# Storing GpSimd's FFN blocks from GpSimd's own DMA queue, in a two-layer hybrid trunk

## The chip, the cores and the metric

The kernel runs on one core of one Trainium2 chip. The metric is the device time of one execution in microseconds, as the median of several runs; lower is better. The core has TensorE (matmuls), VectorE, ScalarE and GpSimd, called PE, DVE, ACT and POOL in the profile, and SyncE (SP), which computes nothing and issues DMAs from its queue in order.

## The reference, cut to what matters

Two decoder layers work on x of 1024 tokens by 1024 channels, in float32. Each has a mixer (layer 0: Mamba-2 heads and latent attention; layer 1: gated linear attention and sparse attention) and then the feed-forward network (FFN) which the change touches:

```python
FFN_HIDDEN = -(-8 * D_MODEL // (3 * 256)) * 256      # 2816

def swiglu(h, w_gate, w_up, w_down):
    return (jax.nn.silu(h @ w_gate) * (h @ w_up)) @ w_down

for layer in range(DEPTH):
    ...
    h = rmsnorm(x, pre_f) * (1.0 + scale_f) + shift_f
    x = x + gate_f * rmsnorm(swiglu(h, *ffns[layer]), post_f)
```

## The kernel before, in words

**Precision.** Each float32 operand of a large product is split into a high and a low part, and a product is three matmuls (`mm3`, L111 to L116): high by high, high by low, low by high. A "product" below is twelve matmuls: four slices of the contraction, three each.

**The FFN's first half** (`ffn`, L1285). Gate and up (`mt` 0 and 1) are multiplied by the seven-product scheme of Strassen and Winograd over quarters: 2816 hidden rows are eleven pairs of 128 (`pm` 0 to 10, `NM` is 11), and each pair has seven products, named "1" to "7", for each of gate and up. They run in the order 1, 6, 2, 7, 5, 4, 3, gate before up in each. For the first five pairs (`HEADS`) products 1 and 2 are taken earlier, and their u blocks wait in DRAM (`uq`), so later those pairs take only ten products each, the others fourteen.

**Weights.** `advance`, called ahead of each product, does what is due. It loads raw weights (`load`, L1347: tiles `rawa`, four buffers, and `raw`, two buffers, the latter for the "b" half), forms their sums on VectorE (`presum`, L1353 to L1355, and one more at L1369), and splits them into high and low (`wpair`, L1333 on ScalarE and L1334 on VectorE). A `raw` buffer comes free when L1334 has read its last weight.

**Results.** A product ends in a PSUM bank, which VectorE adds to a block of 128 by 512 (tile `blk`, ten buffers): L1530, L1535, L1545, L1555 and L1565 for products 6, 7, 4, 5 and 3. SiLU is on ScalarE (L1547, L1557, L1567), and gate times up of products 4 and 5 on GpSimd (L1549, L1559). After product 3 of up, `finish` (L1483) makes the last four blocks with five operations (L1489, L1491, L1493, L1495, L1497), on GpSimd for all pairs but the last, on VectorE for the last. Each finished block is stored to the DRAM tensor `hid`, seven blocks a pair: block 0 at L1396 (made by VectorE), block 1 at L1550, block 4 at L1560, and four in `store` (L1486) in `finish`.

**The second half** (`ffn_out`, L1603) is also in seven passes. It reads `hid` back block by block (L1635) with quarters of the down weight (L1636); what it needs of sums of the down weight is formed in the first half by `down_sums`, a background stream.

**Order.** The program is written for a tile framework, which works out the semaphores and the buffers. A planner orders each engine's instructions ahead of time, by the order of the program and its own estimate of when each could start; on the chip each engine's queue then runs strictly in that order. SP's queue holds all loads and stores, so what stands behind a store waits until that store's block is made. Background streams (the modulation vectors, L257 and L276, and `down_sums`) are pinned to the order of the program.

Of the kernel before, what the change touches and what calls it, by code (L numbers as in the profile page):

```python
# [46 lines left out]
class Trunk:  # L47
# [1237 lines left out]
    def ffn(self, l, near, far, ew):  # L1285


        nc, I, m = self.nc, self.I, self.mod
        S = self.S
        tt, ptt = nc.vector.tensor_tensor, nc.gpsimd.tensor_tensor  # L1290
        hid = self.t(self.dram, [7, self.NM, P, 512], "hid")
# [12 lines left out]
        def product(ps, w, c, b, start):  # L1304

            for k in range(4):
                cs = slice(c * 512 + k * P, c * 512 + (k + 1) * P)
                self.mm3(ps, w[0][:, cs], w[1][:, cs], b[0][:, k, :], b[1][:, k, :], start and k == 0, k == 3, True)
# [71 lines left out]
        def first(mt, pm, w):  # L1380

            ps = self.cx()
            product(ps, w, 0, B[0], True)
            u = blk()
            nc.scalar.copy(u, ps)  # L1385
            return ps, u

        def second(mt, pm, w, ps):

            product(ps, w, 1, B[1], False)  # L1390
            if mt == 0:
                c = cblk[pm] = blk()
                nc.scalar.activation(c, ps, AF.Silu)
            else:
                tt(cblk[pm], cblk[pm], ps, op=ALU.mult)
                nc.sync.dma_start(hid[0, pm], cblk.pop(pm) if pm < self.HEADS else cblk[pm])  # L1396
# [32 lines left out]
        def wkey(pm, mt, p):  # L1429
            return pm, mt, "h" if pm < self.HEADS and p in "12" else WT[p]  # L1430
# [17 lines left out]
        def advance(t):  # L1448

            while loads and free[home(*loads[0])]:  # L1450
                free[home(*loads[0])] -= 1
                load(*loads.pop(0))
            def presums():
                while sums and need[sums[0][1], sums[0][0], 1] - t <= 10:
                    mt, pm = sums[0]
                    if (mt, pm, "b") not in raws or pm >= self.HEADS and (pm, mt, 0) not in W:
                        break
                    presum(*sums.pop(0))

            presums()  # L1460
            while todo and need[todo[0]] - t <= 6:
                place = places[turns[0]]
                if place in user and last[user[place]] >= t:
                    break
                pm, mt, j = key = todo[0]
                if j == "h":
                    if (mt, pm, "h") not in raws:
                        break
                elif (mt, pm, "a") not in raws or j and (mt, pm) in sums:
                    break  # L1470
                todo.pop(0)
                user[place] = key
                W[key] = prep(mt, pm, j)
                if j == 0:
                    presums()
                if j == 2:
                    free["b"] += 1
                if j == 3:
                    free["a"] += 1
                if j == "h":  # L1480
                    free[home(mt, pm, j)] += 1

        def finish(pm, g, u, u3, c21):  # L1483

            def store(n, v):
                nc.sync.dma_start(hid[n, pm], v)  # L1486
            ptt = tt if pm == self.NM - 1 else nc.gpsimd.tensor_tensor
            h11, h21, h22, h12 = cblk.pop(pm), c21, u3, u
            ptt(h12, h12, g["u"], op=ALU.mult)  # L1489
            s1, s2, s3 = g["u"], g["c21"], g["u3"]  # L1490
            ptt(s1, h12, h22, op=ALU.add)  # L1491
            store(5, s1)
            ptt(s2, s1, h11, op=ALU.subtract)  # L1493
            store(2, s2)
            ptt(s3, h11, h12, op=ALU.subtract)  # L1495
            store(3, s3)
            ptt(h12, h21, s2, op=ALU.subtract)  # L1497
            store(6, h12)

        def reload(pm):  # L1500
            for mt in range(2):
                u = ublk[mt, pm] = blk()
                nc.sync.dma_start(u, uq[mt, pm])
# [4 lines left out]
        for t, (pm, mt, p) in enumerate(seq):  # L1508
            advance(t)
            if t > 16 and t % 4 == 0:  # L1510
                self.pump()
            if len(seq) - t in (7, 6, 5, 4, 2):
                next(out)
            st = state.setdefault((pm, mt), {})
            w = W.get(wkey(pm, mt, p))
            if p == "1":
                st["x"], u = first(mt, pm, w)
                if pm < self.HEADS:
                    nc.sync.dma_start(uq[mt, pm], u)
                else:  # L1520
                    ublk[mt, pm] = u
            elif p == "2":
                second(mt, pm, w, st["x"])
                if mt and pm == self.HEADS - 1:
                    reload(0)
            elif p == "6":
                ps = self.sm()
                product(ps, w, 0, T["2"], True)
                u = ublk[mt, pm]
                tt(u, u, ps, op=ALU.add)  # L1530
            elif p == "7":
                ps = st["z"] = self.bk()
                product(ps, w, 1, T["3"], True)
                st["u3"] = blk()
                tt(st["u3"], ublk[mt, pm], ps, op=ALU.add)  # L1535
            elif p == "4":
                if mt == 0 and pm < self.HEADS:
                    cblk[pm] = blk()
                    nc.sync.dma_start(cblk[pm], hid[0, pm])
                if mt and pm + 1 < self.HEADS:  # L1540
                    reload(pm + 1)
                ps = st["z"]
                product(ps, w, 1, T["4"], False)
                c = st["c21"] = blk()
                tt(c, ublk[mt, pm], ps, op=ALU.add)  # L1545
                if mt == 0:
                    nc.scalar.activation(c, c, AF.Silu)  # L1547
                else:
                    ptt(c, c, state[pm, 0]["c21"], op=ALU.mult)  # L1549
                    nc.sync.dma_start(hid[1, pm], c)  # L1550
            elif p == "5":
                ps = st["v"] = self.bk()
                product(ps, w, 0, T["1"], True)
                c = st["u3"]
                tt(c, c, ps, op=ALU.add)  # L1555
                if mt == 0:
                    nc.scalar.activation(c, c, AF.Silu)  # L1557
                else:
                    ptt(c, c, state[pm, 0]["u3"], op=ALU.mult)  # L1559
                    nc.sync.dma_start(hid[4, pm], c)  # L1560
            else:
                ps = st["v"]
                product(ps, w, 0, T["b"], False)
                u = ublk[mt, pm]
                tt(u, u, ps, op=ALU.add)  # L1565
                if mt == 0:
                    nc.scalar.activation(u, u, AF.Silu)  # L1567
                    state[pm, 0]["u"] = u
                else:
                    g = state.pop((pm, 0))  # L1570
                    finish(pm, g, u, st["u3"], st["c21"])
                    state.pop((pm, 1))
            if t in (0, 2, 4, 6, 8, 9, 12, 16):
                next(gen)
# [928 lines left out]
```

## Time and profile before

| what | value |
|---|---|
| median of 3 runs | 3119.78 us |
| lowest and highest of them | 3115.93 and 3125.87 us |
| the profiled execution's own time | 3123.05 us |
| its span, from first to last instruction | 3121.3 us |
| mean granted TensorE clock in it | 0.985 |

The profiled execution lies 3.27 us above the median and within the runs shown; 1.75 us of its time lie outside the span. Durations in the next sections come from that one execution. In timelines a row has the start and the length in microseconds, then engine, line, operation and tiles written and read; "[2.77 <-DVE blk L1535]" says that the engine was idle 2.77 us before the row and what ended it. "q" behind an engine's name is its queue, which waits and issues DMAs. Rows of waits say who waited for whom, the total in microseconds, how often, and the longest.

### The profile page before, as it was taken

What the parts mean: (1) busy time and instruction counts of PE and PEld (TensorE: products, weight loads), DVE (VectorE), ACT (ScalarE), POOL (GpSimd) and SP (SyncE); (2) the same over time, 40 slices, a digit from 0 to 9 for tenths busy, and PEclk for the clock granted to TensorE, in tenths of its full rate; (3) what the DMA queues carried; (4) which work ended last, traced back from release to release, by engine and by line L of the source; (5) the groups of instructions that cost most, each with busy time, mean ns of one, the idle gap of its engine ahead of it and who ended that gap; (6) DMA issues with size and microseconds to landing.
All of it is one profiled execution on the core that took longest, in us unless ns stands there. A gap on an engine that the chain in (4) does not pass through costs nothing. (4 is left out here: it accounts for less than half of the span.)

```text
span 3121.3 us, 43059 instructions
## 1 busy us (share of the span) xinstructions
PE 3009.7 (96%) x15880; PEld 2437.7 (78%) x15880; DVE 2161.1 (69%) x3381; ACT 1338.6 (43%) x2193; POOL 699.0 (22%) x671
## 2 busy tenths in 40 slices
PE   7999999999999999999999999899999999999998
PEld 6887877777787888887888888767777787888787
DVE  5876856768777787667546554687766887777655
ACT  6445444546522223435432432355555732223433
POOL 1003343101034222001213422022222124222001
PEclk9999999999999999999999999999999999999999
DMA  6567432325554556974434334331313645455864
GB/s 224 167 213 223 146 119 96 101 68 197 186 176 159 195 197 234 317 253 153 147 109 156 129 103 133 117 112 57 97 51 105 234 162 195 175 190 198 291 195 161
DMA packets 222866, 510.16 MB, mean 163 GB/s; under 512 B 23824, under 2 KB 62832, under 8 KB 221632
## 3 DMA queue, kind: packets, MB, share of 16 engines
q1 hardware_dynamic: 222656, 507.42, 48.6%
q8 instruction: 125, 2.05, 0.3%
q14 instruction: 85, 0.70, 0.1%
HBM read 370.09 MB, written 137.25 MB: 163 GB/s over the span
## 5 line engine op out<-in xcount | busy, mean ns | idle before, releaser
L115 PE MATMUL bk<-slab,whi 128*128 128x512 f32 x1176 | 467.3, 397 | 1.9 <-DVE slab L145 1.9
L114 PE MATMUL bk<-slab,whi 128*128 128x512 f32 x752 | 312.4, 415 | 6.7 <-ACT whi L132 5.5
L116 PE MATMUL bk<-slab,wlo 128*128 128x512 f32 x752 | 298.1, 397 | 0.0
L115 PEld LDWEIGHTS bk<-slab,whi 128*128 128x128 f32 x1176 | 224.2, 191 | 50.8 <-issue 2.9
L114 PE MATMUL bk<-T,whi 128*128 128x512 f32 x528 | 210.0, 398 | 2.9 <-DVE blk L1535 1.7
L116 PE MATMUL bk<-T,wlo 128*128 128x512 f32 x528 | 207.7, 393 | 0.0
L151 POOL TENSOR_SCALAR rstd<-ss 128x1 f32<-128x1 f32 (+1 forms) x86 | 28.9, 336 | 712.0 <-ACT junk L158 651.7
L114 PEld LDWEIGHTS bk<-slab,whi 128*128 128x128 f32 x752 | 144.7, 192 | 41.3 <-issue 6.2
L116 PEld LDWEIGHTS bk<-slab,wlo 128*128 128x128 f32 x752 | 144.3, 192 | 31.4
L1333 ACT ACTIVATE whi<-rawa 128x512 fp32r<-128x512 f32 (+1 forms) x108 | 80.4, 750 | 194.0 <-PE bk L115 160.8
L114 PE MATMUL cx<-slab,whi 128*128 128x512 f32 x368 | 146.2, 398 | 6.5 <-ACT blk L1385 3.9
L2316 POOL TENSOR_SCALAR pexp<-pexp,rs 128x640 f32<-128x640 f32 (+7 forms) x128 | 95.8, 752 | 246.2 <-DVE rs L2315 91.5
L115 PE MATMUL cx<-slab,whi 128*128 128x512 f32 x368 | 145.1, 394 | 0.2 <-DVE slab L397 0.2
L116 PE MATMUL cx<-slab,wlo 128*128 128x512 f32 x368 | 144.9, 394 | 0.0
L1116 PE MATMUL sm<-ident,pexp 128*128 128x128 f32 x816 | 132.4, 278 | 7.1 <-POOL pexp L2316 2.3
L1559 POOL TENSOR_TENSOR blk<-blk,blk 128x512 f32<-128x512 f32 x22 | 35.3, 1602 | 419.2 <-DVE blk L1555 306.9
L1116 PEld LDWEIGHTS sm<-ident,pexp 128*128 128x128 f32 x816 | 93.4, 140 | 44.9 <-issue 19.7
L1118 ACT COPY pT<-sm 128x512 f32<-128x512 f32 (+2 forms) x144 | 76.4, 531 | 112.5 <-PE sm L1116 111.4
L1334 DVE TENSOR_TENSOR wlo<-rawa,whi 128x512 fp32r<-128x512 f32 (+1 forms) x108 | 118.1, 1094 | 7.3 <-ACT whi L1333 6.7
L114 PEld LDWEIGHTS bk<-T,whi 128*128 128x128 f32 x528 | 99.2, 188 | 28.7 <-DVE blk L1535 2.2
L2312 ACT ACTIVATE pexp<-pexp,nm 128x640 f32<-128x640 f32 (+7 forms) x128 | 94.0, 734 | 61.5 <-DVE nm L2310 46.3
L1650 DVE TENSOR_TENSOR slab<-ab,slab 128x1024 fp32r<-128x1024 f32 x66 | 80.7, 1223 | 54.1 <-ACT slab L1649 51.8
(660 smaller groups left out, 8590.2 us busy)
## 6 DMA issues: line engine op xcount, KB each, us to landing
ada<-in_l_ada_w_dram SPq DMA_DIRECT2D x80, 512.0 KB, 4.4
hid<-blk SPq DMA_DIRECT2D x154, 256.0 KB, 2.0
raw<-in_l_w_in_dram SPq DMA_DIRECT2D x48, 512.0 KB, 3.6
ab<-hid SPq DMA_DIRECT2D x94, 256.0 KB, 2.7
cat<-cat SPq DMA_DIRECT2D x64, 256.0 KB, 2.7
ab<-wt SPq DMA_DIRECT2D x60, 256.0 KB, 5.4
raw<-in_l_w_gate_dram SPq DMA_DIRECT2D x28, 512.0 KB, 4.9
raw<-in_l_w_up_dram SPq DMA_DIRECT2D x28, 512.0 KB, 4.1
```

The source lines that it names most:

```text
L114: mm(out, lh, rh, start=start, stop=False, skip_group_check=more)
L115: mm(out, lh, rl, start=False, stop=False, skip_group_check=more)
L116: mm(out, ll, rh, start=False, stop=stop, skip_group_check=more)
L151: nc.gpsimd.tensor_scalar(r, ss, inv_d, EPS, op0=ALU.mult, op1=ALU.add)
L1116: nc.tensor.transpose(ps[:, k * P:(k + 1) * P], e[:, (b + k) * P:(b + k + 1) * P], self.ident)
L1118: (nc.scalar.copy if self.evac else nc.vector.tensor_copy)(pt[:, b:b + m, :], ps[:, :m * P].rearrange("p (k c) -> p k c", c=P))
L1333: nc.scalar.activation(hi, src, AF.Copy)
L1334: (eng or nc.vector).tensor_tensor(lo, src, hi.bitcast(F32), op=ALU.subtract)
L1559: ptt(c, c, state[pm, 0]["u3"], op=ALU.mult)
L1650: tt(lo, r, hi.bitcast(F32), op=ALU.subtract)
L2312: nc.scalar.activation(e, e, AF.Exp, bias=nm, scale=-1.0, accum_out=rs)
L2316: nc.gpsimd.tensor_scalar(e, e, rs, 0.0, op0=ALU.mult, op1=ALU.add)
```

## The change

Stores of blocks that GpSimd makes are issued by GpSimd itself and no longer by SP: in `finish` for all pairs but the last, whose blocks VectorE makes and SP still stores, and at products 4 and 5 of up for every pair. Block 0 stays on SP. No arithmetic changes. Line numbers behind it rise by three.

```diff
         def finish(pm, g, u, u3, c21):
 
+            on_vector = pm == self.NM - 1
+            queue = nc.sync if on_vector else nc.gpsimd
+
             def store(n, v):
-                nc.sync.dma_start(hid[n, pm], v)
-            ptt = tt if pm == self.NM - 1 else nc.gpsimd.tensor_tensor
+                queue.dma_start(hid[n, pm], v)
+            ptt = tt if on_vector else nc.gpsimd.tensor_tensor
...
                     ptt(c, c, state[pm, 0]["c21"], op=ALU.mult)
-                    nc.sync.dma_start(hid[1, pm], c)
+                    nc.gpsimd.dma_start(hid[1, pm], c)
...
                     ptt(c, c, state[pm, 0]["u3"], op=ALU.mult)
-                    nc.sync.dma_start(hid[4, pm], c)
+                    nc.gpsimd.dma_start(hid[4, pm], c)
```

## The prediction

> **What bounds the kernel now.** I read the page first, then the windows of the two FFN product stages, then TensorE's own gaps inside them, and last what VectorE and the SP queue waited for just before each gap. The page:
>
> ```profile
> PE 3009.7 (96%) x15880; PEld 2437.7 (78%) x15880; DVE 2161.1 (69%) x3381; ACT 1338.6 (43%) x2193; POOL 699.0 (22%) x671
> ...
> q1 hardware_dynamic: 222656, 507.42, 48.6%
> ...
> hid<-blk SPq DMA_DIRECT2D x154, 256.0 KB, 2.0
> ```
>
> TensorE is busy 96% of the span, so a stall elsewhere counts only where it reaches TensorE. All the program's own DMAs run on one hardware queue; 154 of them store an FFN block. The change moves 124 of these. The windows (span, then PE, PEld, DVE, ACT, POOL busy, clock, DMA share) of the two stages in which those stores are made:
>
> ```profile
> 850.00:1210.00 360.00, 355.86 (x1526) 285.74 (x1524) 278.34 (x327) 103.33 (x145) 118.38 (x70) 1.00 0.52 182
> 2490.00:2870.00 380.00, 374.23 (x1610) 302.51 (x1609) 299.78 (x345) 113.75 (x158) 118.75 (x70) 1.00 0.52 180
> ```
>
> TensorE is idle 4.1 us in the first and 5.8 us in the second: 9.9 us together. Closing gaps can win no more in these stages, but for what a gap does to the matmuls behind it. TensorE's own timeline (start, length, idle before it) has the gaps:
>
> ```profile
> 957.32 0.50 PE L114 MATMUL bk<-T,slab 128*128 128x512 f32 x1 [2.77 <-DVE blk L1535]
> ...
> 2587.12 0.40 PE L115 MATMUL bk<-slab,whi 128*128 128x512 f32 x1
> 2587.35 0.39 PE L116 MATMUL bk<-T,wlo 128*128 128x512 f32 x1
> 2589.49 0.50 PE L114 MATMUL bk<-T,whi 128*128 128x512 f32 x1 [1.74 <-DVE blk L1535]
> ...
> 2620.94 0.50 PE L114 MATMUL bk<-T,slab 128*128 128x512 f32 x1 [3.29 <-DVE blk L1535]
> ...
> 2622.39 0.63 PE L116 MATMUL bk<-T,slab 128*128 128x512 f32 x1
> 2622.82 0.63 PE L114 MATMUL bk<-T,slab 128*128 128x512 f32 x1
> ```
>
> Matmuls normally start 0.23 us apart (2587.12, 2587.35). Three gaps, all released by L1535, VectorE's reading of a finished bank. After the last one they start 0.43 us apart (2622.39, 2622.82). Now why L1535 was late, in VectorE's timeline at the three places:
>
> ```profile
> 949.66 1.18 DVE L1334 TENSOR_TENSOR wlo<-rawa,whi 128x512 fp32r<-128x512 f32 x1
> 954.53 0.69 DVE L1353 TENSOR_TENSOR raw<-raw 128x512 f32<-128x512 f32 x1 [3.69 <-DMA raw<-in_l_w_up_dram]
> ...
> 2570.65 1.21 DVE L1334 TENSOR_TENSOR wlo<-raw,whi 128x1024 fp32r<-128x1024 f32 x1
> ...
> 2580.33 0.68 DVE L1334 TENSOR_TENSOR wlo<-rawa,whi 128x512 fp32r<-128x512 f32 x1
> 2587.41 0.69 DVE L1353 TENSOR_TENSOR raw<-raw 128x512 f32<-128x512 f32 x1 [6.41 <-DMA raw<-in_l_w_up_dram]
> 2588.14 0.69 DVE L1354 TENSOR_TENSOR rawa<-raw,rawa 128x512 f32<-128x512 f32 x1
> 2588.75 0.68 DVE L1535 TENSOR_TENSOR blk<-blk,bk 128x512 f32<-128x512 f32 x1
> ...
> 2613.18 1.19 DVE L1334 TENSOR_TENSOR wlo<-rawa,whi 128x512 fp32r<-128x512 f32 x1
> 2618.14 0.69 DVE L1353 TENSOR_TENSOR raw<-raw 128x512 f32<-128x512 f32 x1 [3.77 <-DMA raw<-in_l_w_up_dram]
> ```
>
> Each time VectorE stands, 3.7 to 6.4 us, at the first of the weight sums (L1353) for an up weight that has not landed, and L1535 is queued behind it. The SP queue at the same places (start, length; merged rows hold several stores):
>
> ```profile
> 944.67 5.97 SPq L1486 DMA_DIRECT2D hid<-blk  x4
> 950.73 0.38 SPq L1347 DMA_DIRECT2D raw<-in_l_w_up_dram  x1
> ...
> 2569.55 0.33 SPq L1347 DMA_DIRECT2D raw<-in_l_w_gate_dram  x1
> 2575.28 5.44 SPq L1486 DMA_DIRECT2D hid<-blk  x4
> ...
> 2581.29 0.39 SPq L1347 DMA_DIRECT2D raw<-in_l_w_up_dram  x1
> ...
> 2608.20 5.97 SPq L1486 DMA_DIRECT2D hid<-blk  x4
> 2614.26 0.38 SPq L1347 DMA_DIRECT2D raw<-in_l_w_up_dram  x1
> ```
>
> The load goes out right behind the four stores of `finish`. At the middle place its buffer was free when VectorE had read the last weight out of it, 2570.65 + 1.21 = 2571.86, but it was issued at 2581.29: 9.4 us late, while SP stood at stores whose blocks GpSimd had not finished. What SP waited for in the first stage (us in total, times, longest):
>
> ```profile
> SPq L1486 <- POOL blk L1491: 59.8, 10, 8.0
> SPq L1550 <- POOL blk L1549: 37.0, 10, 5.1
> SPq L1560 <- POOL blk L1559: 34.5, 10, 6.3
> ```
>
> **The change part by part.** *Stores taken off SP.* Per layer: four in `finish` for ten of eleven blocks and one each at the two products for all eleven, 62, so 124. SP saves 124 issues of 0.32 us (row below), 40 us, and waits like the three rows above, 131 us in one stage. Neither is on the path by itself; SP is no bound. What counts is the load behind: the three L1353 waits go if it lands 3.7 to 6.4 us sooner, and at the middle place there are 9.4 us to take.
>
> *TensorE's three gaps.* By starts less the normal 0.23: the first counts as its idle 2.77 plus about 0.16 of modelled overlap, 2.9; the second 2589.49 - 2587.35 - 0.23 = 1.9; the third 3.29 plus the same 0.16, 3.45. Behind the third, some seven matmuls at 0.43 instead of 0.23: 1.4. Sum 9.7 us: 7.8 of the 9.9 idle, 0.5 of overlap and the 1.4; the other 2.1 of idle have other causes and stay.
>
> *What is late next.* With the weight there, VectorE goes on at once. Three sums at about 0.69 and L1535 at 0.68 make 2.75 us. At the middle place: 2581.01 + 2.75 = 2583.8, and TensorE wants it at 2587.58; 3.8 to spare. At the first: 950.84 + 2.75 = 953.6, wanted at 957.32 - 2.93 = 954.4; 0.8 to spare. At the last: 2614.37 + 2.75 = 2617.1, wanted at 2620.94 - 3.45 = 2617.5; 0.4 to spare. So they close, the last just so. I take 9 of the 9.7.
>
> *Stores put on GpSimd's queue.* No DMA is issued by GpSimd in this trace. The nearest rows, a store from SP, and GpSimd's own pass over one block (ns, least/median/most), then GpSimd's chain in `finish` (first and last of five) and a later row of VectorE:
>
> ```profile
> L1486 SPq DMA_DIRECT2D hid<-blk x88: 319/320/459, 883.3 to 2904.9; - x88
> L1559 POOL TENSOR_TENSOR blk<-blk,blk x22: 1281/1308/2237, 868.4 to 2890.7; 128x512 f32<-128x512 f32 x22
> ...
> 2570.87 2.15 POOL L1489 TENSOR_TENSOR blk<-blk,blk 128x512 f32<-128x512 f32 x1 [3.63 <-DVE blk L1565]
> ...
> 2578.74 1.63 POOL L1497 TENSOR_TENSOR blk<-blk,blk 128x512 f32<-128x512 f32 x1
> ...
> 2597.05 0.68 DVE L1545 TENSOR_TENSOR blk<-blk,bk 128x512 f32<-128x512 f32 x1
> ```
>
> An issue costs GpSimd between 0.32 and 2.24 us; I take 1.0, between them, since it must wait for its own last write as well as issue. GpSimd has 118.38 busy in 360; 60 stores add 19 to 134 us, and it stays under 71%. So no bound. Behind a store on this queue stand only GpSimd's later passes, and for their results nothing waits but stores and the reuse of the ten `blk` buffers. The chain of `finish` takes 2580.37 - 2570.87 = 9.5 us; with four issues 10.8 to 18.5, plus 2.0 to land. One block later, seven blocks are held from the old one and nine are asked for up to L1545 at 2597.05, 26.2 us after the chain began; the last is asked for 5.7 us after the worst case. Cost 0; if an issue took over 3.7 us, VectorE would wait there.
>
> A page bears on this price: the Trainium skill, DMA: Bandwidth & Descriptors, section Latency and other measured facts, gives about 1 us to the first byte on the GpSimd path and 0.6 on SP's. By it the sum would not change; no run here shows it yet.
>
> *The other stores.* hid[0], the spare u blocks and all of the last block's four stay on SP. The last block's two product stores move; they are read only in the second and later of the seven passes behind. Cost 0.
>
> *Order.* The planner sets the order of every queue from its own estimate, and GpSimd's longer chain changes what it sees, in the FFN and behind. No row prices that. The gaps it could open are like those seen, 1.9 to 3.5 us each; one or two either way, minus 5 to plus 5. I take 0.
>
> Sum against the profiled execution: 3123.05 - 9 = 3114. That execution lies 3.3 us above the median of 3119.78, so against the median it is 3111. I forecast 3112.
>
> **The rivals.**
>
> *Nothing moves.* Loads land sooner, but something else stands in front of L1535: the sums have 0.4 and 0.8 us to spare at two of three places, and a SP wait for another buffer could take the place of the stores. Then at most the middle gap closes, 2 us: 3118. The Trainium skill speaks for this case: DMA: Bandwidth & Descriptors, section Issuing engines are not separate DMA queues, says that starting DMAs from several engines only saves the time to start them, usually small. By that rule the gain would be the 0.32 us issues, which are off the path: 3120. The rows above disagree as far as they go, as what SP lost was not issue time but 59.8 us at one wait.
>
> *Slower: GpSimd's issues hold VectorE up.* The two engines already disturb each other:
>
> ```profile
> L1369 DVE TENSOR_TENSOR rawa<-raw,rawa x44: 676/694/1789, 837.9 to 2859.5; 128x512 f32<-128x512 f32 x44
> ...
> sum 120.00, PE 114.93 PEld 91.79 DVE 97.08 ACT 28.93 POOL 49.57; mean PE 38.31 PEld 30.60 DVE 32.36 ACT 9.64 POOL 16.52
> ```
>
> One VectorE sum takes 0.69 us, or up to 1.79 beside a GpSimd pass. If a store's issue cost VectorE the same 1.1, six stores add 6.6 us for each block. The second row sums 2540 to 2660, the part in which five blocks take ten products of twelve matmuls each, 27.6 us: VectorE has 114.93 - 97.08 = 17.9 to spare there, 4.1 per block. So TensorE would lose 2.5 for each of ten such blocks, 25, and the gaps that close give back 9: 3119.8 + 16 = 3136. It decides from 0.7 us a store (4.1 / 6) upward; it is slower than now from about 0.85, and by over 0.3% from 1.0. Against it: an issue does not read the blocks, the pass does. The Trainium skill (SBUF: State Buffer, section Who interferes with whom) has VectorE's sums of two inputs contend only with GpSimd instructions that read; the two lengths of L1369 agree with the first half, and of the second no row here can tell.
>
> *More than forecast.* SP's earlier issue also brings the loads of the next stage forward; worth perhaps 5 us more: 3107.
>
> **How the numbers follow.** Gaps close: 0.50, around 3112, its own range 3107 to 3117. Nothing moves: 0.28. Slower: 0.15. More: 0.07. A measurement of this kernel tells about 0.3% from no change, 9.4 us: faster is below 3110.4, slower above 3129.1. A little under half of the first case lies below 3110.4, 0.23, and all of the last: faster 0.30. Most of the slower rival lies above: 0.13, with 0.02 for an unlucky order: 0.15. Same 0.55. The range takes in the last case and part of the slower rival: 3103 to 3127.
>
> **What would show it.** Right: no L1353 wait over 2 us for the up weight; no L1486 on SP except the last block's; the first stage at under 1 us of idle TensorE. GpSimd's issues between 0.3 and 2.2 us. Wrong: L1369 and its like at 1.7 us more often than now, VectorE over 90% busy in 2540 to 2660, waits for a `blk` buffer at L1535 or L1545, or gaps of TensorE at new lines.

## The result and the profile after

| | median, us | runs |
|---|---|---|
| before, on the same chip | 3119.41 | 6, from 3113.28 to 3125.87 |
| after | 3103.62 | 6, from 3099.36 to 3108.78 |

The ratio is 0.9947, 95% interval 0.9934 to 0.996: the change saves 16.5 us (12.5 to 20.6), where 7.8 were forecast. The prediction's kind of effect was there, about twice as large.

The page of the changed kernel, lines that answer to those shown of before:

```profile
PE 2999.9 (97%) x15880; PEld 2433.5 (79%) x15880; DVE 2175.6 (70%) x3381; ACT 1339.4 (43%) x2193; POOL 748.3 (24%) x795
...
q1 hardware_dynamic: 204800, 474.91, 45.9%
q0 software_dynamic: 9920, 32.51, 2.8%
...
hid<-blk POOLq DMA_DIRECT2D x124, 256.0 KB, 2.5
```

The 124 stores are now in a queue of their own kind (q0), 32.51 MB, and land 2.5 us after their issue, not 2.0. The windows of the two FFN stages (columns as before):

```profile
850.00:1210.00 360.00, 360.00 (x1545) 289.82 (x1544) 291.71 (x336) 104.28 (x147) 144.79 (x130) 1.00 0.54 188
2490.00:2870.00 380.00, 380.00 (x1646) 308.77 (x1645) 307.84 (x353) 114.49 (x159) 146.84 (x132) 1.00 0.55 189
```

TensorE has no idle time left in either; before, it had 4.1 and 5.8 us. VectorE is busier by 13.4 and 8.1 us, at no cost; in part this is because the windows are fixed in time and nine and eight more of its instructions now fall into them. Its waits for the up weight, each time the row of the window 850 to 1210 and then that of 2490 to 2870 (total, times, longest), before:

```profile
DVE raw L1353 <- DMA raw<-in_l_w_up_dram: 20.9, 6, 6.9
...
DVE raw L1353 <- DMA raw<-in_l_w_up_dram: 21.9, 7, 6.4
```

and after:

```profile
DVE raw L1353 <- DMA raw<-in_l_w_up_dram: 1.7, 2, 1.1
...
DVE raw L1353 <- DMA raw<-in_l_w_up_dram: 2.4, 5, 0.8
```

That is the prediction's first step, as foreseen. At its middle place the load was issued 9.4 us after its buffer came free. The rows for the same weight in the changed kernel:

```profile
2557.43 1.23 DVE L1334 TENSOR_TENSOR wlo<-raw,whi 128x1024 fp32r<-128x1024 f32 x1
...
2558.68 0.33 SPq L1347 DMA_DIRECT2D raw<-in_l_w_up_dram  x1
```

The buffer is free at 2557.43 + 1.23 = 2558.66, and the load goes out at 2558.68. What the prediction's sum did not hold lies behind the windows, where the second half of the FFN takes over. Timelines of SP and of VectorE there in layer 1, before:

```profile
2860.73 5.99 SPq L1486 DMA_DIRECT2D hid<-blk  x4
2866.81 0.38 SPq L1593 DMA_DIRECT2D ada<-in_l_w_down_dram  x1
...
2867.74 0.42 SPq L1635 DMA_DIRECT2D rawa<-hid  x1
...
2870.89 0.69 DVE L1589 TENSOR_TENSOR ada<-ada 128x512 f32<-128x512 f32 x1 [2.24 <-DMA ada<-in_l_w_down_dram]
```

and after:

```profile
2831.77 0.33 SPq L1596 DMA_DIRECT2D ada<-in_l_w_down_dram  x1
...
2846.07 0.33 SPq L1638 DMA_DIRECT2D rawa<-hid  x1
...
2849.51 0.68 DVE L1592 TENSOR_TENSOR ada<-ada 128x512 f32<-128x512 f32 x1
```

The four stores of the tenth pair's `finish` stood ahead of the down weight's loads too. They are gone from SP, this load of `ada` goes out 35 us earlier (19 of them because the whole kernel is ahead by then), and VectorE no longer waits for it. The last pair's four stay on SP, as the change says, and the load of `ada` behind them is still waited for: 5.0 us at 2888.05, 6.0 before.

To see where time goes without the noise of whole executions, I take from each trace the time between the same matmuls, counted in order of start: from number 4420 to 5960 is layer 0's first FFN half, 5960 to 6420 its handover to the second half, 13260 to 14900 and 14900 to 15330 the same in layer 1. "Sum" is the four stages less the mean of the two executions of before; "measured" is (ratio - 1) times 3119.4 us, with its interval.

| kernel | FFN 0 | handover 0 | FFN 1 | handover 1 | sum | measured |
|---|---|---|---|---|---|---|
| before, and again as control | 363.8, 363.9 | 107.0, 108.3 | 386.5, 387.1 | 105.3, 103.7 | 0 | 0 |
| after | 359.4 | 103.1 | 379.7 | 100.2 | -20.4 | -16.5 (-20.6 to -12.5) |
| again | 359.4 | 103.2 | 379.1 | 102.4 | -18.7 | -16.8 (-20.9 to -12.8) |
| heads | 359.4 | 107.0 | 379.7 | 104.7 | -12.0 | -12.5 (-16.5 to -8.7) |
| tails | 364.2 | 105.7 | 385.3 | 102.0 | -5.6 | -1.6 (-4.4 to 1.2) |
| spfirst | 359.3 | 104.9 | 379.1 | 100.1 | -19.4 | -16.8 (-20.3 to -13.1) |
| double | 359.4 | 108.2 | 379.4 | 106.0 | -9.8 | -10.0 (-13.7 to -6.2) |
| tiny | 359.4 | 103.7 | 379.6 | 101.4 | -18.7 | -14.7 (-20.3 to -9.4) |
| wtonly | 359.4 | 111.7 | 379.1 | 104.6 | -8.0 | -7.5 (-11.5 to -3.4) |
| lastonly | 359.4 | 107.2 | 379.7 | 105.4 | -11.1 | -10.3 (-13.7 to -6.6) |
| allstores | 359.4 | 112.9 | 379.8 | 112.8 | 2.1 | -0.3 (-3.4 to 2.8) |

The stages are of one execution of each kernel; in the change, again, spfirst and tiny their sums say 2 to 4 us more than the medians. The load of `ada` shown above goes with the handover's time: it goes out 12.6 us (layer 0) and 13.3 us (layer 1) ahead of the matmul at which the handover begins in before, in control and in heads, and 26.4 to 29.6 us ahead in the change, again, tails, spfirst and splate. The handovers take at least 107.0 and 103.7 us in the first three and at most 105.7 and 102.4 in the others.

Outside the four stages the profiled executions differ by several us with no pattern: layer 1 up to its FFN took 1169.4 us in the first execution of before, 1166.5 in the control and 1165.4 after. That is how the two profiled executions came to lie 23.7 us apart, 3123.05 and 3099.36.

### The profile page after: what moved, and what is told of

Read it like the earlier page. It is cut to its first block, busy times and chain, and to the rows that moved or that the text cites. A ratio compares the mean times of both kernels' runs of the same rounds, so it can differ in the third digit from the quotient of the medians.

```text
span 3097.7 us, 43064 instructions
## 1 busy us (share of the span) xinstructions
PE 2999.9 (97%) x15880; PEld 2433.5 (79%) x15880; DVE 2175.6 (70%) x3381; ACT 1339.4 (43%) x2193; POOL 748.3 (24%) x795
## 3 DMA queue, kind: packets, MB, share of 16 engines
q0 software_dynamic: 9920, 32.51, 2.8%
```

## The experiments

The theory: SP's queue runs in order, and `finish`'s stores in it wait for GpSimd's passes, so the loads behind them go out late; any way of taking the stores out of the loads' way brings the gain. Rivals: that it is GpSimd's own issuing that helps, that another wait was removed, and that the handover's part is chance.

**control: the kernel before, once more.**

> The kernel before, once more, for a second profile of it. If the 3 to 5 us that the mixers of layer 1 differ between the two profiles at hand is only the difference of one execution from another (each engine's order is the same there), then this profile's mixers differ from the first one's by as much; its TensorE gaps in the FFN should be the same as the first one's: behind L1535 near 957, 2589 and 2621, and 4 to 5 us at the handover to the second half of layer 1.

It took 3121.33 us. Its gaps, from TensorE's timeline, here the last:

```profile
2620.24 0.50 PE L114 MATMUL bk<-T,slab 128*128 128x512 f32 x1 [2.87 <-DVE blk L1535]
```

The three gaps behind L1535 are at the same products, and so is a gap at layer 0's handover. Layer 1's handover is 1.6 us shorter than in the first execution, so its share is known only to a few us. A gap of 1.4 us at 990.67 in the first execution is not here, and yet the stage takes as long. After the first gap TensorE here ran at half its clock for a while, as the clock column (the third from the end) shows, first in this run and then, after the same gap, in the first execution of before:

```profile
959.40:962.80 3.40, 3.40 (x9) 2.63 (x9) 3.37 (x5) 1.52 (x3) 2.19 (x1) 0.50 0.51 154
...
957.80:961.20 3.40, 3.40 (x17) 2.71 (x16) 3.40 (x6) 1.47 (x3) 1.99 (x1) 1.00 0.42 154
```

The two losses are alike in size, and tails has the gap (at 989.58) and not the slow clock; that one takes the other's place is likely, not shown.

**heads and tails: the change for some pairs only.** Pairs 0 to 4 have ten products each, 5 to 10 have fourteen.

```diff
-            queue = nc.sync if on_vector else nc.gpsimd
+            queue = nc.gpsimd if not on_vector and pm < self.HEADS else nc.sync
```

The two product stores are treated alike (not shown). tails has `>=` in place of `<`; the last pair's four stay on SP.

> Only the first five pairs of each layer (ten products each) store from GpSimd, the other six as before. Two-places theory: the gaps behind L1535 and the one at the gate (990) close, 11 us by the two profiles, and the gaps at the handover to the second half stay, 9 us: about 3109 to 3111, ratio 0.997. Rival, all of the gain is in these pairs and the handover only shifted by chance: the full 16 us, 3103, ratio 0.9947.

> Only the last six pairs (fourteen products each) store from GpSimd. Two-places theory: the three gaps behind L1535 stay as before, and the gaps at the handover shrink by about 4 us in layer 0 and 5 us in layer 1: 3110 to 3113, ratio 0.9975. Rival, handover by chance: no change, 3119.

heads: 3106.84 us against 3117.97, ratio 0.996 (0.9947 to 0.9972). tails: 3118.07, ratio 0.9995 (0.9986 to 1.0004). VectorE's waits for the up weight in the two windows, of heads:

```profile
DVE raw L1353 <- DMA raw<-in_l_w_up_dram: 1.8, 2, 0.9
...
DVE raw L1353 <- DMA raw<-in_l_w_up_dram: 1.9, 4, 1.2
```

and of tails, with its last gap of TensorE:

```profile
DVE raw L1353 <- DMA raw<-in_l_w_up_dram: 23.1, 7, 7.0
...
DVE raw L1353 <- DMA raw<-in_l_w_up_dram: 19.1, 7, 5.5
...
2616.18 0.50 PE L114 MATMUL bk<-T,slab 128*128 128x512 f32 x1 [3.34 <-DVE blk L1538]
```

So nearly all of the gain in the FFN stages comes from the stores of the first five pairs, and none of the handover's does: heads keeps both handovers at the time of before. heads came out faster than its 3109 to 3111. tails missed its 3110 to 3113: the handovers shorten by 2.0 and 2.5 us in one execution, where the change has 4.5 and 3.2, and its median is that of the rival, no change. That the handover is part of the gain rests on the stages and on the load of `ada`, not on these two times.

**splate: the stores stay on SP, but later.** The stores of `finish`, for all pairs but the last, are issued two products later, and they and all raw-weight loads (L1347) are pinned to the program's order.

```diff
-            nc.sync.dma_start(r, src)
+            self.pin(nc.sync.dma_start(r, src))
...
+        late, LATE = [], 2
...
-                nc.sync.dma_start(hid[n, pm], v)
+                if pm == self.NM - 1:
+                    nc.sync.dma_start(hid[n, pm], v)
+                else:
+                    late.append((t + LATE, hid[n, pm], v))
...
+            while late and (late[0][0] <= t or t + 8 > len(seq)):
+                self.pin(nc.sync.dma_start(*late.pop(0)[1:]))
```

> All stores stay on SP; in finish they are only put behind the load of the next up weight (two products later in the program, with these loads and stores kept in the order of the program). Theory, what stands ahead of the load in SP's queue is the cause and GpSimd's queue is only one way out: the three gaps behind L1535 close as with the change, about 9 us, and the handover stays: 3109 to 3112, ratio 0.997. Rival, it matters that the stores run on another DMA queue and not who waits in front of the load: no gain or a loss, 3119 or more, with the waits at L1353 still there.

3122.32 us, ratio 1.0009 (0.9998 to 1.002). The time is the rival's, and yet the theory did not fall: the waits for the up weight go (the longest is 2.1 us), and the four stages took 359.4, 103.8, 378.9 and 100.5 us, as in the change. The pin of every load put the first loads of each FFN behind work that they need not wait for, and new gaps opened at its start, in layer 1:

```profile
2496.49 0.80 PE L114 MATMUL cx<-slab,whi 128*128 128x512 f32 x1 [6.60 <-ACT whi L1333]
```

In both layers the granted clock was 0.50 for 10.2 us around this gap (from 825.5 and from 2494.6), which adds to it. The stretches from the first matmul to number 4420 and from 6420 to 13260 are 15 us longer each than in before (857.3 and 1182.6 against means of 842.3 and 1168.0; the profiled execution, 3132.18 us, was the longest of its 11). The experiment carried a second change that ate the first; the next one leaves it out.

**again and spfirst: the change once more, and the same without GpSimd's queue.** spfirst puts `finish`'s stores two products later on SP, as splate does, and pins only these and the "b" loads behind the first pair.

```diff
+            ins = nc.sync.dma_start(r, src)
+            if which == "b" and pm:
+                self.pin(ins)
...
+                    late.append((t + LATE, hid[n, pm], v))
...
+            while late and (late[0][0] <= t or t + 8 > len(seq)):
+                self.pin(nc.sync.dma_start(*late.pop(0)[1:]))
```

> The changed kernel once more, for a direct comparison and a second profile: ratio 0.993 to 0.996, 3103 us. If the handover is part of the gain, TensorE's gaps between 1200 and 1270 sum to under 1 us again, and those between 2840 and 2920 to about 2 us; if they come out near the 2.7 and 3.6 us of the second profile of the kernel before, the handover was one execution's luck.

> All stores stay on SP; finish's are put two products later in the program, and only they and the loads of the b halves from the second pair on are kept in the order of the program, so that the loads at the start of the FFN keep their places. If what stood ahead of the up load is the cause, the three gaps behind L1535 close as with the first five pairs' stores on GpSimd: 9 to 12 us, 3106 to 3110, ratio 0.9965, and the waits of 7 to 9 us at the start of each FFN that the other kernel with late stores showed are gone. If the other DMA queue matters, the waits at L1353 stay and the time too, 3118.

again: 3101.22 us against 3118.68, ratio 0.9946 (0.9933 to 0.9959). TensorE has no gap in again's first handover and one of about 2 us in its second, so the handover was not one execution's luck. spfirst: 3100.25, ratio 0.9946 (0.9935 to 0.9958), faster than the 3106 to 3110 expected, because the handovers shorten as well: the load of `ada` now stands ahead of the late stores.

```profile
2832.67 0.38 SPq L1602 DMA_DIRECT2D ada<-in_l_w_down_dram  x1
...
2840.41 5.96 SPq L1518 DMA_DIRECT2D hid<-blk  x4
```

spfirst's page has the DMAs of before, all 154 stores from SP, and its windows' waits for the up weight those of the change (the sum's line is L1355 here):

```profile
hid<-blk SPq DMA_DIRECT2D x154, 256.0 KB, 2.2
...
DVE raw L1355 <- DMA raw<-in_l_w_up_dram: 1.8, 4, 1.0
...
DVE raw L1355 <- DMA raw<-in_l_w_up_dram: 2.3, 4, 1.3
```

SP still waits for GpSimd in this kernel; the longest rows of SP's waits, 850 to 1210, are

```profile
SPq L1559 <- POOL blk L1558: 45.1, 10, 5.5
SPq L1569 <- POOL blk L1568: 40.9, 10, 6.1
SPq L1518 <- POOL blk L1498: 36.7, 9, 7.0
```

and no harm comes of it, because the loads that VectorE needs next stand ahead of these stores. This is the experiment that decides: what mattered is what stands behind a waiting store, not which engine issues it nor how long SP waits in all.

One rival is left, the order of VectorE. The planner moved the sums of the up weight in every kernel that has the FFN stages' gain, in the same 24 places in the change, again, heads, double and tiny, and tails has the order of before. spfirst speaks against it: at the second of the three places all three sums of the up weight stand right ahead of the second L1535 (here L1544), where two of them stood before, and there is no wait and no gap of TensorE:

```profile
2566.17 0.68 DVE L1355 TENSOR_TENSOR raw<-raw 128x512 f32<-128x512 f32 x1
...
2568.70 0.68 DVE L1544 TENSOR_TENSOR blk<-blk,bk 128x512 f32<-128x512 f32 x1
```

No kernel has the early loads with all of the old order.

**double and tiny: the price of GpSimd's issues.** In double, each store by GpSimd is followed by a second one of the same block to a spare tensor; in tiny, by one of its first 16 columns.

```diff
                 queue.dma_start(hid[n, pm], v)
+                if not on_vector:
+                    queue.dma_start(spare[n, pm], v)          # tiny: v[:, :16]
```

> As the change, but each block that GpSimd stores is stored a second time, to a spare tensor that nobody reads: 124 more issues on GpSimd, 32.5 MB more to DRAM. If an issue costs GpSimd 0.56 us and nobody else anything, the time is the changed kernel's, 3103, ratio 0.995. If issues hold VectorE up by 1.1 us each, six more a pair cost 6.6 us a pair against 4.1 to spare in the ten short pairs: 25 us more, 3128. If a block's buffer held longer is the limit, waits for blk appear at L1538 or L1548.

> The change, and each GpSimd store is followed by a second one from GpSimd that writes only the first 16 of the 512 columns to a spare tensor: 124 issues more, but 1 MB instead of 32.5. Theory A, the issues are what cost 8.5 us when every store was made twice (GpSimd busy longer, VectorE's passes beside them longer): 3107 to 3111, ratio about 0.997, and VectorE again some 17 us busier than in the change. Theory B, it was the bytes, which delayed other transfers at the handover (the load behind the wt store went out 6.5 us after it instead of 3.1): 3100 to 3104, ratio about 0.995, gaps at the handover as in the change.

double: 3109.74 us against 3118.68, ratio 0.9968 (0.9956 to 0.998); again, on the same chip, had 3101.22. tiny: 3105.08 against 3120.47, ratio 0.9953 (0.9935 to 0.997). GpSimd's issues (ns, least/median/most), in the change and then in double:

```profile
L1489 POOL DMA_DIRECT2D hid<-blk x80: 539/557/1047, 884.6 to 2847.6; - x80
L1563 POOL DMA_DIRECT2D hid<-blk x22: 580/580/772, 869.7 to 2870.0; - x22
...
L1492 POOL DMA_DIRECT2D spare<-blk x80: 539/539/548, 884.5 to 2856.6; - x80
```

VectorE's busy time in tiny's two windows:

```profile
850.00:1210.00 360.00, 360.00 (x1544) 289.46 (x1544) 298.13 (x334) 105.78 (x147) 176.44 (x190) 1.00 0.56 190
2490.00:2870.00 380.00, 379.75 (x1644) 307.92 (x1643) 315.62 (x352) 112.75 (x157) 176.45 (x190) 1.00 0.57 191
```

14.2 us more than in the change for 118 more issues, 0.12 us each. TensorE hardly notices: 0.25 us of idle in the second. The time of double went at the handovers (table), and the DMA view suggests how: 22 stores of `wt`, and SP's 30 of hid (KB each, median us to landing), of again:

```profile
wt<-ada SPq DMA_DIRECT2D x22, 512.0 KB, 3.4
wt<-adaacc SPq DMA_DIRECT2D x22, 512.0 KB, 3.3
...
hid<-blk SPq DMA_DIRECT2D x30, 256.0 KB, 3.3
```

and of double:

```profile
wt<-ada SPq DMA_DIRECT2D x22, 512.0 KB, 4.0
wt<-adaacc SPq DMA_DIRECT2D x22, 512.0 KB, 4.1
...
hid<-blk SPq DMA_DIRECT2D x30, 256.0 KB, 4.9
```

In tiny the two `wt` rows have 3.4 and 3.0 us, but the row of `hid` has 4.3, so that one does not part bytes from issues. That it is the bytes rests on the `wt` landings and on the handovers, one execution each (103.7 and 101.4 us in tiny, as in the change); by their times alone the two kernels' intervals overlap.

**allstores, wtonly, lastonly: every store from GpSimd, and which of them.** allstores moves hid[0], the last pair's four and the down weight's sums (`wt`) as well; wtonly moves only the `wt` stores on top of the change, lastonly only the others.

```diff
-            queue = nc.sync if on_vector else nc.gpsimd
+            queue = nc.gpsimd                                  # allstores, lastonly
...
-                nc.sync.dma_start(hid[0, pm], ...)
+                nc.gpsimd.dma_start(hid[0, pm], ...)           # allstores, lastonly
...
-                nc.sync.dma_start(wt[k, pm], r)
+                nc.gpsimd.dma_start(wt[k, pm], r)              # allstores, wtonly
```

> As the change, and all other stores of hid (block 0 of every pair, the last pair's four) and the stores of the down weight's sums (wt) also go from GpSimd. If SP's waits for unfinished blocks still cost at the handover, its remaining gaps, about 2 us a layer, shrink: 1 to 4 us less than the change, 3100 to 3102, ratio 0.9938. If these stores now wait behind GpSimd's own passes and free their buffers later, the loads of the down weight come later and the handover grows: 2 to 6 us more than the change.

> The change, and the two stores of each weight-difference step (wt) from GpSimd as well; nothing else. It shares out what was lost when all stores went to GpSimd (3119.1 against 3101.2). Theory A, the wt stores lose it, since the two buffers behind them come free later and SP's next load of them (L1596) stands ahead of the down projection's loads: 3112 to 3119. Rival B, the last block's stores lose it, since reads of hid wait for GpSimd's queue: 3100 to 3104 here.

> The change, and hid[0] and the last block's four stores from GpSimd as well; wt stays on SP. Theory A, the wt stores lose it: 3100 to 3105. Rival B, the last block's stores lose it, since the first loads of the down projection wait until GpSimd's last store has landed: 3111 to 3119, with TensorE's gaps at 1252 to 1268 and 2904 to 2924 as when all stores went to GpSimd.

allstores: 3119.09 us against 3118.68, ratio 0.9999 (0.9989 to 1.0009), the whole gain lost. wtonly: 3115.15 against 3120.47, ratio 0.9976 (0.9963 to 0.9989). lastonly: 3110.91, ratio 0.9967 (0.9956 to 0.9979). Neither theory was right alone: against the change wtonly loses about 9 us and lastonly about 6, together nearly what allstores loses. All of it is at the handovers. SP's longest wait in wtonly's first (1222 to 1258), and what TensorE has of it:

```profile
SPq L257 <- DMA wt<-ada: 6.3, 1, 6.3
...
1264.78 0.77 PE L114 MATMUL sm<-slab 128*128 128x512 f32 x1 [5.96 <-DVE uacc L1708]
```

The load into `ada` waits in SP's queue until the `wt` store out of it has landed, and the down projection's loads stand behind. In lastonly (2868 to 2905) a read of `hid` waits for a store of it:

```profile
SPq L1638 <- DMA hid<-blk: 2.2, 1, 2.2
...
2894.93 0.50 PE L114 MATMUL sm<-x 128*128 128x512 f32 x1 [3.08 <-ACT x L1652]
```

In allstores that wait is 5.9 us. In all three VectorE's order at the handovers differs from the change's as well; how the loss is shared between the waits and the order is open. In wtonly the clock adds to the gap: it is 0.50 from 1262.8 to 1269.6, and TensorE is busy in 4.8 us of that, so some 2.4 us are lost.

## Why the prediction was wrong in size and right in kind

**The sum.** This step failed. It was made over the windows 850 to 1210 and 2490 to 2870 alone, and what happens behind them stood at nothing in it; it appeared only as the rival "More than forecast", 5 us with a chance of 0.07. The table has 4.5 and 3.2 us for the two handovers (means of after and again against the two of before), 7.7 in all, and the traces show the mechanism that the rival named: the stores stood ahead of the next stage's loads. The medians leave less for it: the 16.5 us saved less 11.9 of the FFN stages is 4.6, so its size is known only as 4.6 to 7.7. The row that could have told it, four stores taking 5.99 us directly ahead of the down weight's loads at 2860.73, lay inside the last window.

**TensorE's three gaps.** Right in cause, too small in size: 9 us taken, 11.9 measured (4.45 in layer 0, 7.4 in layer 1). "The other 2.1 of idle have other causes and stay" was wrong, as both windows are now full; 1.4 of it was the gap at 990.67, which waited for VectorE's L1545. And in the control a run of eight matmuls at 0.43 instead of 0.23 us followed the first gap as well, 1.6 us that were counted only behind the third. The prediction did not say what these slow matmuls are: the granted clock was 0.50 there, as shown for the control, and behind the third gap of before as well:

```profile
2622.00:2625.40 3.40, 3.40 (x10) 2.62 (x9) 3.40 (x5) 1.78 (x3) 2.19 (x1) 0.50 0.47 154
```

**What is late next.** Right in outcome; the margins of 0.8, 3.8 and 0.4 us were not put to the test. They were worked out with VectorE's order of before, and the planner moved the sums ahead. No wait for the up weight is over 1.1 us. The sum that waited 3.69 us at 954.53 before is now made here, with no wait (the tenth run of L1353 in both):

```profile
945.29 1.89 DVE L1353 TENSOR_TENSOR raw<-raw 128x512 f32<-128x512 f32 x1
```

**Stores put on GpSimd's queue.** An issue takes 0.54 to 0.58 us (medians) where 1.0 was taken, and VectorE's rows of waits show none for a `blk` buffer. Landing takes 2.5 us, where SP's stores took 2.0 in before and 2.2 in spfirst. The Trainium skill (DMA: Bandwidth & Descriptors, section Latency and other measured facts) has first bytes at about 1 us and 0.6 us, a difference of 0.4 by estimate; the 0.5 and 0.3 us longer landings here agree with that.

**Order.** Taken at 0; it opened no new gap, and what it was worth is not shown by itself (see spfirst). VectorE's order changed in 24 places, all in short pairs, with sums of the up weight moved ahead of the reading of a bank. Some of them now run beside GpSimd's passes, which is part of why VectorE is busier:

```profile
L1353 DVE TENSOR_TENSOR raw<-raw x44: 679/692/1780, 805.6 to 2842.6; 128x512 f32<-128x512 f32 x44
...
L1353 DVE TENSOR_TENSOR raw<-raw x44: 683/693/2425, 806.0 to 2822.8; 128x512 f32<-128x512 f32 x44
```

The first row is of before, the second of after: the median is the same, the longest is not.

**The rivals.** "Nothing moves" fell with the waits. The rule that stood beside it (the Trainium skill, DMA: Bandwidth & Descriptors, section Issuing engines are not separate DMA queues), that issuing from several engines saves only the time to issue, is half borne out: spfirst shows that a second engine was not needed, but the 16.8 us that it saves are not issue time, since it issues as many DMAs from SP as before. "Slower" asked for 0.7 us of VectorE for each store. The change has 599.6 us of VectorE in the two windows and spfirst, with all stores on SP, has

```profile
850.00:1210.00 360.00, 360.00 (x1545) 289.46 (x1544) 284.30 (x336) 105.82 (x147) 118.32 (x70) 1.00 0.54 189
2490.00:2870.00 380.00, 380.00 (x1646) 308.51 (x1645) 298.77 (x353) 114.36 (x159) 121.02 (x72) 1.00 0.54 190
```

583.1: 16.5 us for 120 stores, 0.14 us each, a fifth of what would decide. With gaps and handovers the sum would have been 11.9 + 7.7 = 19.6 us by the stages, 3119.8 - 19.6 = 3100.2 from the median that the prediction went by. The measured saving is 16.5, and its interval, 12.5 to 20.6, holds both.

## What to carry to other kernels

In a queue that runs in order, a store whose data is not ready is priced by the loads behind it, not by its own wait: look for every load that follows it, up to the next stage, and not only for the one whose wait is largest. The remedy is the order; another engine's queue is one way to it, issuing the store a little later is another that costs no engine time, and moving every store costs the gain again if reads and buffer reuse then wait for them. When a sum is made over windows, look also at what the same cause does just behind their edges.

## What the hardware showed that was not expected

A store issued by GpSimd occupies it 0.54 to 0.58 us, and as long whether it moves 256 KB or 8 KB of a block (539 and 537 ns at L1492 in double and in tiny; GpSimd is busy 176.4 us in a window of tiny and 176.5 in double). It goes with 0.12 to 0.14 us more of VectorE's busy time; whether the issue itself or passes that now run side by side cost that is not shown. 32.5 MB of additional stores, spread over the two FFN halves, lengthened the `wt` stores' median landing from 3.4 to 4.0 us and made the two handovers 8.6 us longer than again's, where 124 issues with 1 MB did not.

A gap of TensorE could cost more than its length. Behind some of them the granted clock was 0.50 for 3.4 us, 1.7 us lost: in control behind the gap of 2.9 us at 958.0, in heads behind one of 2.0 us at 1259.63. Behind the same gap at 957.32 in before it was 1.00.
